# A second norm behind one block instead of two, three squares on another engine, and three pads that shift every working tile in SBUF

## The chip, the cores and the metric

The kernel runs on one core of a Trainium2 chip. The metric is device microseconds (us) of one execution. The engines are TensorE (PE, whose weight loads the profile lists apart as PEld), VectorE (DVE), ScalarE (ACT), GpSimd (POOL), and SyncE (SP), which here only issues DMAs. Each works off its own queue in order.

## The reference

One layer of a decoder trunk on x of 1024 positions and 1024 channels, all in float32:

```python
h = rms_norm(x, norm_mix_pre)
z = h @ w_in                                   # pool, query, RWKV and gate columns
merged = gates[0]*y_pool + gates[1]*y_rwkv + gates[2]*y_mem
x = x + rms_norm(merged @ w_o, norm_mix_post)  # the residual of the mixer
h = rms_norm(x, norm_ffn_pre)
u = causal_dwconv(h @ w_ffn_up, conv_w, conv_b)
u_gate, u_val = split(u)
f = (gelu(u_gate) * u_val) @ w_ffn_down
x = x + rms_norm(f, norm_ffn_post)
```

y_pool is causal pooling, y_rwkv a recurrence over 16 heads (run here in chunks of 64 positions), y_mem attention into 256 memory tokens.

## The kernel before

Everything is transposed: channels on the 128 partitions, positions along a row, in two halves of 512 positions. Each float32 operand is split into a high part, rounded to the format that TensorE takes at its fast rate (FR, float32r), and a low part, the remainder. A product is three matmuls (`mm3`, L167 to L169): high weights by high rows, high weights by low rows, low weights by high rows, each 128x128 by 128x512. A block is one 128-channel output over all 1024 input channels: 8 pieces of 128 channels, so 24 such matmuls into one bank of PSUM (`psg`).

Weights come in pieces of 128x256 (`load_w`, `load_more`): SP loads `wraw`, ACT casts it to `whi` (L128), POOL subtracts to get `wlo` (L131). There are two classes of buffers, used by turns, each with 3 `wraw`, 4 `whi` and 4 `wlo`; a block is four pieces.

The stages, by time in the trace: up to about 100 us the first norm of x; to about 1000 us the input projection (rows `hh`, `hl`) as filler between the small matmuls of the recurrence; then attention, and the projections of the branches (rows `oh`/`ol`, `ph_`/`pl_`, `yh`/`yl`), the merge (`mgh`/`mgl`) and the output projection `wo_gemm`; from about 1380 us the first FFN blocks one by one on rows `h2h`/`h2l`; from about 1510 to 1850 us the other FFN blocks in pairs (`up_pair`: seven products of 12 matmuls into banks `psf`, with weights `wt` and rows `h2h`/`h2l` or differences `t`); then the down projection (banks `psd`, weights `u`, rows `f`).

Around the change, for the second half of the positions: `wo_gemm(1, ...)` makes eight output blocks. Of each, VectorE copies the bank to the tile `o` (L1116), ScalarE squares the bank (L1090), and VectorE adds the square into `ss` (L1091). `wo_residual(1, ...)` has one matmul with `ones` sum `ss` over the channels (`norm`, L1096, into `psn`), ScalarE takes a logarithm and an exponential (L199, `rs`), and then for each of eight rows VectorE scales (L1134) and adds x (L1136), ScalarE squares, and VectorE adds into `s2` (L1091, `s` in the trace). It is a generator that stops after every second row. `wo_norm(1, ...)` sums `s2` by another L1096 matmul, scales again and splits into `h2h[1]`, `h2l[1]`. While this runs, TensorE makes the blocks of the FFN on the first half: `first(0)`, `first(NF)`, `first(1)`, `first(NF + 1)`, `first(2)`, `first(NF + 2)`, called f0, g0, f1, g1, f2, g2 below. Each is evacuated by `conv`: ACT (L961), then two DVE operations and a tiny copy (L962, L963, L965). The L1096 matmuls are pinned behind the matmul that was last when they were written.

SBUF is given out in pools. `const`, `wp` (weights, staging) and the pools of each stage (`rw`, `at`, `ow`, `fa` and others) are stacked from the low end; `hp`, `pmp`, `hf`, `yp` and others from the high end. What a matmul reads lies, in the program as built, at these places modulo 256 bytes (all offsets inside these tiles are multiples of 256):

| operands | before | after |
|---|---|---|
| `whi`, `wlo` (pool `wp`) | 192 | 224 |
| `hh`, `hl`, `yh`, `yl`, `mgl`, `h2h`, `h2l` (high end) | 224 | 224 |
| `mgh`, `oh`, `ol`, `ph_`, `pl_` | 64 | 224 |
| `wt` of `up_pair`: two of every six products in `ow`, the other four in `pmp` | 64, 224 | 224, 224 |
| `t` of `up_pair`: `T1`, `T2` in `at`, `T3` in `pmp` | 64, 64, 224 | 224 |
| `u`, `f` of the down projection (pool `at`) | 64 | 224 |
| `ones`, `ident`, `bonesr`, `cent` (`const`) | 192 | 192 |

Of the 512-wide three-matmul products, 3776 matmuls read weights at 192 and rows at 224 (2784 with `hh`/`hl`, 480 with `h2h`/`h2l`, 384 with `yh`/`yl`, 128 with `mgl`), 640 weights at 192 and rows at 64 (`mgh`, `oh`, `ol`, `ph_`, `pl_`), and of the 1428 into `psf` 648 read weights and rows at different places, 780 at the same. All 876 into `psd` read both at 64.

Of the kernel before, what the change touches and what calls it, by code (L numbers as in the profile page):

```python
# [9 lines left out]
F32 = mybir.dt.float32  # L10
FR = mybir.dt.float32r
AF = mybir.ActivationFunctionType
ALU = mybir.AluOpType
# [4 lines left out]
P = 128  # L18
# [10 lines left out]
NF = 22  # L29
# [15 lines left out]
def trunk_kernel(ctx: ExitStack, tc: tile.TileContext, xT, memT, pvec, w_in, w_kv, w_upd, w_upg,  # L45
                 w_pool, w_ppool, w_pmem, w_prwkv, w_o, w_fup, w_fdn, out):
    nc = tc.nc
    V, A, G, PE, SP = nc.vector, nc.scalar, nc.gpsimd, nc.tensor, nc.sync

    const = ctx.enter_context(tc.tile_pool(name="const", bufs=1))  # L50
# [54 lines left out]
                        base=-1, channel_multiplier=-1)  # L105
    G.memset(smask, 1.0)
    G.memset(smask.rearrange("p (c s) -> p c s", s=C)[:, :, 0:1], 0.0)
    eps = const.tile([P, 3], F32, name="eps")
    for j, e in enumerate((NORM_EPS, L2_EPS, LNX_EPS)):
        G.memset(eps[:, j:j + 1], e)  # L110
# [190 lines left out]

    def shifted(m, dst):

        zc = wp.tile([P, 1], F32, name="zc", tag="zc", bufs=4)

        def evac(t0, ps):
            d = dst[:, t0:t0 + 512]
            A.activation(d, ps, AF.Identity, scale=omu[:, m:m + 1])
            if t0 == 0:
                V.tensor_copy(zc, ps[:, 511:512])  # L310
            else:
                V.scalar_tensor_tensor(d[:, 0:1], zc, col("mu", m), d[:, 0:1], op0=ALU.mult,
                                       op1=ALU.add)
            V.scalar_tensor_tensor(d[:, 1:512], ps[:, 0:511], col("mu", m), d[:, 1:512],  # L314
                                   op0=ALU.mult, op1=ALU.add)
        return evac
# [532 lines left out]
    for hd in range(4):  # L849
        for t0, _ in HALVES:  # L850
            s = slice(t0, t0 + 512)
            q = as_.tile([P, 512], F32, name="q", tag="q", bufs=2)
            SP.dma_start(q, d_zq[hd][:, s])
            qh = as_.tile([P, 512], FR, name="qh", tag="qh")
            ql = as_.tile([P, 512], FR, name="ql", tag="ql")
            split(q, qh, ql, V)
            po = pss.tile([P, 512], F32, name="po", tag="s")
            for u in range(2):
                ps = psg.tile([P, 2, 256], F32, name="psco", tag="g0")
                for tt in range(2):  # L860
                    ts_ = slice((2 * u + tt) * P, (2 * u + tt + 1) * P)
                    mm3(ps[:, tt], (qh[:, ts_], ql[:, ts_]), (kh[:, hd], kl[:, hd]), True, True)
                mx = as_.tile([P, 8], F32, name="mxs", tag="mxs", bufs=2)
                V.reduce_max(mx[:, 0:2], ps, axis=AX.X)
                V.tensor_scalar(mx[:, 2:4], mx[:, 0:2], -SC, None, op0=ALU.mult)
                pr = as_.tile([P, 2, 256], F32, name="prb", tag="prb", bufs=2)
                for tt in range(2):
                    act(pr[:, tt], ps[:, tt], AF.Exp, bias=mx[:, 2 + tt:3 + tt], scale=SC,
                        accum_out=mx[:, 4 + tt:5 + tt])
                V.reciprocal(mx[:, 6:8], mx[:, 4:6])  # L870
                V.tensor_tensor(pr, pr, mx[:, 6:8].unsqueeze(2).broadcast_to([P, 2, 256]), op=ALU.mult)
                pt = (psc if u else psk).tile([P, 2, 2, P], F32, name="ptr", tag="c" if u else "k")
                for tt in range(2):
                    for m in range(2):
                        PE.transpose(pt[:, m, tt], pr[:, tt, m * P:(m + 1) * P], ident)
                pth = as_.tile([P, 2, 256], FR, name="pth", tag="pth", bufs=2)
                ptl = as_.tile([P, 2, 256], FR, name="ptl", tag="ptl")
                split(pt.rearrange("p m t s -> p m (t s)"), pth, ptl, V)
                for m in range(2):
                    mm3(po[:, u * 256:(u + 1) * 256], (vh[:, hd, m], vl[:, hd, m]), (pth[:, m], ptl[:, m]),  # L880
                        m == 0, m == 1)
            split(po, oh[hd][:, s], ol[hd][:, s], V)
        pool_products(hd)
        if hd < 2:
            pool_sums(hd + 2)
        for j, ev in fill[2 * hd:2 * hd + 2]:
            in_block(j, ev, 1)
# [197 lines left out]
    def sumsq(acc, src, first, eng):  # L1085
        if first:
            A.activation(acc, src, AF.Square)
        else:
            sq = wp.tile([P, 512], F32, name="sq", tag="st", bufs=3)[:, :src.shape[-1]]
            A.activation(sq, src, AF.Square)  # L1090
            eng.tensor_tensor(acc, acc, sq, op=ALU.add)  # L1091
# [13 lines left out]
    def wo_gemm(n, js):  # L1105
        s = slice(n * 512, n * 512 + 512)
        for j in js:
            if j == 0:
                o = [(ow if n == 0 else ow1).tile([P, 2, 512], F32, name="o", tag=f"q{4 * n + a}") for a in range(4)]
                os_.append([o[k // 2][:, k % 2] for k in range(KC)])  # L1110
                sss.append(ow.tile([P, 512], F32, name="ss", tag="ss", bufs=2))
            rhs = lambda k: (mgh[k][:, s], mgl[n][k])
            if n == 1 and j == 0:
                two.extend(two_gemms([load_w(w_o[e], KC) for e in range(2)], rhs, KC - 1))
            ps = two.pop(0) if two else gemm(load_w(w_o[j], KC), rhs)
            V.tensor_copy(os_[n][j], ps)  # L1116
            sumsq(sss[n], ps, j == 0, V)

    def wo_residual(n, after=None):

        s = slice(n * 512, n * 512 + 512)
        o = os_[n]
        rs = norm(ow, sss[n], after)
        s2 = ow.tile([P, 512], F32, name="s2", tag="ss", bufs=2)
        if n:
            xts = hf.tile([P, KC, 512], F32, name="xts", tag="h2h1")
            SP.dma_start(xts, xT[:, s].rearrange("(k p) t -> p k t", p=P))
        for k in range(KC):
            if n:
                xt = xts[:, k]  # L1130
            else:
                xt = ow.tile([P, 512], F32, name="xt", tag="xt", bufs=2)
                SP.dma_start(xt, xT[k * P:(k + 1) * P, s])
            V.scalar_tensor_tensor(o[k], o[k], col("g_mix_post", k), rs, op0=ALU.mult,  # L1134
                                   op1=ALU.mult)
            V.tensor_tensor(o[k], o[k], xt, op=ALU.add)  # L1136
            SP.dma_start(d_x1[k][:, s], o[k])
            sumsq(s2, o[k], k == 0, V)
            if k % 2:
                yield s2  # L1140
# [31 lines left out]
    s2 = next(res)  # L1172
# [12 lines left out]
    def first(j):  # L1185
        return up_block(j, 0, load_w(w_fup[j], KC))

    pairs = [[first(0), first(NF)]]
    res = wo_residual(1, last_mm[0])
    s2 = next(res)  # L1190
    for i in (1, 2):
        pairs.append([first(i)])
        s2 = next(res)
        pairs[i].append(first(NF + i))
        s2 = next(res, s2)

# [412 lines left out]
```

## Time and profile before

| | us |
|---|---|
| median of 3 runs (2083.38 to 2085.0) | 2084.89 |
| profiled execution, its own time | 2084.65 |
| span of its instructions | 2082.7 |
| PE busy (12246 matmul records) | 2026.5, 97% of the span |
| DVE, ACT, POOL busy | 1358.2, 1070.6, 810.8 |
| mean granted TensorE clock | 0.993 |

Of the time of an execution, 1.95 us lie outside the span. The profile says of busy PE that the ends of matmuls are modelled, since they are pipelined: how fast matmuls follow each other is read from the starts of rows in the timeline, not from the duration column.

### The profile page before, as it was taken

To read this page: it belongs to the slowest core of one execution; us is meant where nothing else is said; L and a number is where in the kernel's file an instruction comes from. 1 tells how busy PE (TensorE), PEld (TensorE's weight loads), DVE (VectorE), ACT (ScalarE), POOL (GpSimd) and SP (SyncE) were. 2 spreads that over 40 slices of the span, in tenths; PEclk is the share of its full clock that TensorE was granted. 3 is DMA by queue.
4 is the path that set the end of the run, shared out by engine and by line. 5 is a ranking of instruction groups with operands and counts; after the bars stand their busy time and mean duration, and the time that the engine had idled before them with its cause. 6 is when DMAs were issued, how large, how long until landed. Compare 5 with 4: busy or idle time off the path is not lost.

```text
span 2082.7 us, 34125 instructions
## 1 busy us (share of the span) xinstructions
PE 2026.5 (97%) x12246; PEld 1559.1 (75%) x12246; DVE 1358.2 (65%) x2167; ACT 1070.6 (51%) x2252; POOL 810.8 (39%) x917
## 2 busy tenths in 40 slices
PE   8999999999999999999999999998999999999997
PEld 5777767776778667876878878776778877777886
DVE  6567437664667357833795452769877777777798
ACT  7585348623772368434566243545443444444644
POOL 5521213121222121212122355565578888842341
PEclk9999999999999999999999999999999999999999
DMA  4312211120212021213526443634222222169766
GB/s 155 129 41 74 67 51 67 67 82 22 87 61 89 30 92 44 86 55 120 172 84 223 129 134 107 220 102 151 94 88 83 82 78 76 61 185 273 168 178 152
DMA packets 176713, 221.83 MB, mean 107 GB/s; under 512 B 16544, under 2 KB 128288, under 8 KB 176544
## 3 DMA queue, kind: packets, MB, share of 16 engines
q1 hardware_dynamic: 163616, 204.44, 30.2%
q0 software_dynamic: 11856, 14.16, 4.2%
q8 instruction: 97, 1.59, 0.3%
q10 hardware_dynamic: 1072, 1.05, 0.1%
q14 instruction: 72, 0.59, 0.1%
HBM read 170.30 MB, written 49.28 MB: 105 GB/s over the span
## 4 chain that ended last, share of the span: by engine, by line
PE 36%; DVE 5%; DMA 4%; POOL 3%; issue 2%; ACT 2%; SPq 1%; POOLq 0%; ACTq 0%; DVEq 0%
PE psg L167 6%; PE psg L169 6%; PE psg L168 6%; PE psf L169 3%; PE psf L167 3%; PE psf L168 3%; POOL wt L1027 2%; PE psd L168 2%; PE psd L169 2%; PE psd L167 2%; DMA R<-d_f 1%; POOL sm L1012 1%; DMA a<-in_w_fup 1%; ACT d L1043 1%; DMA fw<-in_w_fdn 1%
## 5 line engine op out<-in xcount | busy, mean ns | idle before, releaser
L131 POOL TENSOR_TENSOR wlo<-wraw,whi 128x256 fp32r<-128x256 f32 x472 | 410.4, 878 | 951.7 <-ACT whi L128 760.2
L167 PE MATMUL psg<-hh,whi 128*128 128x512 f32 x928 | 383.6, 413 | 2.5 <-DVE kv L314 2.5
L169 PE MATMUL psg<-hh,wlo 128*128 128x512 f32 x928 | 379.8, 409 | 0.1
L168 PE MATMUL psg<-hl,whi 128*128 128x512 f32 x928 | 378.8, 408 | 0.0
L128 ACT CAST whi<-wraw 128x256 fp32r<-128x256 f32 x472 | 182.7, 403 | 227.9 <-PE psg L168 122.1
L167 PEld LDWEIGHTS psg<-hh,whi 128*128 128x128 f32 x928 | 174.6, 188 | 46.5 <-DVE kv L314 3.8
L169 PEld LDWEIGHTS psg<-hh,wlo 128*128 128x128 f32 x928 | 174.3, 188 | 45.9 <-POOL wlo L131 5.1
L168 PEld LDWEIGHTS psg<-hl,whi 128*128 128x128 f32 x928 | 174.7, 188 | 42.9 <-issue 3.6
L1027 POOL TENSOR_TENSOR wt<-a,wt 128x256 fp32r<-128x256 f32 x136 | 133.8, 1012 | 30.8 <-ACT wt L1026 30.8
L167 PE MATMUL psd<-f,u 128*128 128x512 f32 x292 | 115.0, 394 | 5.7 <-ACT f L1347 3.4
L168 PE MATMUL psd<-f,u 128*128 128x512 f32 x292 | 115.0, 394 | 1.0 <-DVE f L1351 1.0
L169 PE MATMUL psd<-f,u 128*128 128x512 f32 x292 | 114.3, 393 | 0.4 <-DVE u L1351 0.4
L1027 POOL TENSOR_TENSOR wt<-sm,wt 128x256 fp32r<-128x256 f32 x102 | 106.8, 1067 | 14.6 <-ACT wt L1026 14.6
L169 PE MATMUL psf<-h2h,wt 128*128 128x512 f32 x272 | 108.0, 397 | 0.4 <-POOL wt L1027 0.3
L168 PE MATMUL psf<-h2l,wt 128*128 128x512 f32 x272 | 107.0, 393 | 0.0
L167 PE MATMUL psf<-h2h,wt 128*128 128x512 f32 x272 | 106.8, 393 | 0.0
L1026 ACT CAST wt<-sm 128x256 fp32r<-128x256 f32 x102 | 37.9, 404 | 128.2 <-POOL sm L1012 124.2
L1045 DVE SCALAR_TENSOR_TENSOR d<-z,pv,d 128x1023 f32<-128x1023 f32 x68 | 91.6, 1347 | 12.0 <-ACT d L1043 9.5
L169 PE MATMUL psf<-t,wt 128*128 128x512 f32 x204 | 81.3, 399 | 1.9 <-POOL wt L1027 1.9
L168 PE MATMUL psf<-t,wt 128*128 128x512 f32 x204 | 80.3, 394 | 0.0
L167 PE MATMUL psf<-t,wt 128*128 128x512 f32 x204 | 80.2, 393 | 0.0
L685 DVE TENSOR_TENSOR HV<-ph,Hd 64x128 f32<-64x128 f32 x112 | 32.3, 289 | 71.8 <-PE ph L639 47.7
(422 smaller groups left out, 4751.3 us busy)
## 6 DMA issues: line engine op xcount, KB each, us to landing
wraw<-in_w_in SPq DMA_DIRECT2D x240, 128.0 KB, 2.3
a<-in_w_fup SPq DMA_DIRECT2D x128, 128.0 KB, 2.4
d_zg<-st SPq DMA_DIRECT2D x48, 256.0 KB, 2.7
wraw<-in_w_fup SPq DMA_DIRECT2D x80, 128.0 KB, 2.4
fw<-in_w_fdn SPq DMA_DIRECT2D x33, 256.0 KB, 4.5
fraw<-d_f SPq DMA_DIRECT2D x33, 256.0 KB, 5.2
wraw<-in_w_prwkv SPq DMA_DIRECT2D x64, 128.0 KB, 2.4
wraw<-in_w_o SPq DMA_DIRECT2D x64, 128.0 KB, 2.5
```

The lines of the kernel that those rows point to most:

```text
L128: last_whi[0] = A.copy(hi, src).ins
L131: (V if lo_on_dve[0] else G).tensor_tensor(lo, src, hi.bitcast(F32), op=ALU.subtract)
L167: first = PE.matmul(ps, wh, xh, start=start, stop=False)
L168: PE.matmul(ps, wh, xl, start=False, stop=False)
L169: last_mm[0] = PE.matmul(ps, wl, xh, start=False, stop=stop).ins
L685: ready = V.tensor_tensor(HV[q, :, c + 1, e], ph[q], Hd[q], op=ALU.add).ins
L1012: eng.tensor_tensor(out_[u], a[u], b[u], op=op)
L1026: A.copy(w[0][:, us], src[u])
L1027: last_low[0] = G.tensor_tensor(w[1][:, us], src[u], w[0][:, us].bitcast(F32), op=ALU.subtract).ins
L1043: A.activation(d, z, AF.Identity, scale=col("cw2", j), bias=col("cb", j))
L1045: V.scalar_tensor_tensor(d[:, n:], z[:, :T - n], col(cw, j), d[:, n:], op0=ALU.mult, op1=ALU.add)
```

## The change

Three pads move places in SBUF: an unused tile `cpad` of 32 bytes a partition in `const` (all that follows in `const`, and `wp`, moves up 32 bytes), eight `zc` instead of four (32 bytes each as placed; what is stacked above moves another 128), and 128 bytes instead of 32 for `mxs` (two of them; the tiles of the attention above them move by 352 in all). The table above has the places that follow.

In `wo_gemm`, the squares of output blocks 5, 6 and 7 of the second half are taken by VectorE from the copy `o` in SBUF, not by ScalarE from the bank.

`wo_residual(1, ...)` is started behind f0 instead of behind g0, and its four parts follow f0, g0, f1, g1 instead of g0, f1, g1, f2.

```diff
+    const.tile([P, 8], F32, name="cpad")
...
-        zc = wp.tile([P, 1], F32, name="zc", tag="zc", bufs=4)
+        zc = wp.tile([P, 1], F32, name="zc", tag="zc", bufs=8)
...
-                mx = as_.tile([P, 8], F32, name="mxs", tag="mxs", bufs=2)
+                mx = as_.tile([P, 32], F32, name="mxs", tag="mxs", bufs=2)
...
             V.tensor_copy(os_[n][j], ps)
-            sumsq(sss[n], ps, j == 0, V)
+            if n == 1 and j > 4:
+                sq = wp.tile([P, 512], F32, name="sq", tag="st", bufs=3)
+                V.tensor_tensor(sq, os_[n][j], os_[n][j], op=ALU.mult)
+                V.tensor_tensor(sss[n], sss[n], sq, op=ALU.add)
+            else:
+                sumsq(sss[n], ps, j == 0, V)
...
-    pairs = [[first(0), first(NF)]]
+    pairs = [[first(0)]]
     res = wo_residual(1, last_mm[0])
+    s2 = next(res)
+    pairs[0].append(first(NF))
     s2 = next(res)
     for i in (1, 2):
         pairs.append([first(i)])
-        s2 = next(res)
+        s2 = next(res, s2)
         pairs[i].append(first(NF + i))
         s2 = next(res, s2)
```

TensorE at the norm of the second half, before (`psg_14031` is the bank of g0, `psg_14104` that of f1):

```order
L169 MATMUL psg_14031<-h2h0_13607,wlo_14026 128x512
L167 MATMUL psg_14031<-h2h0_13607,whi_14025 128x512
L168 MATMUL psg_14031<-h2l0_13608,whi_14025 128x512
L169 MATMUL psg_14031<-h2h0_13607,wlo_14026 128x512
L1096 MATMUL psn_14061<-ss_13496,ones_85 128x512
L167 MATMUL psg_14104<-h2h0_13607,whi_14080 128x512
L168 MATMUL psg_14104<-h2l0_13608,whi_14080 128x512
L169 MATMUL psg_14104<-h2h0_13607,wlo_14081 128x512
```

and after (`psg_13977` is the bank of f0, `psg_14050` that of g0; L1097 is the old L1096):

```order
L170 MATMUL psg_13977<-h2h0_13608,wlo_13972 128x512
L168 MATMUL psg_13977<-h2h0_13608,whi_13971 128x512
L169 MATMUL psg_13977<-h2l0_13609,whi_13971 128x512
L170 MATMUL psg_13977<-h2h0_13608,wlo_13972 128x512
L1097 MATMUL psn_14007<-ss_13497,ones_85 128x512
L168 MATMUL psg_14050<-h2h0_13608,whi_14026 128x512
L169 MATMUL psg_14050<-h2l0_13609,whi_14026 128x512
L170 MATMUL psg_14050<-h2h0_13608,wlo_14027 128x512
```

The norm's matmul moved ahead of the 24 matmuls of g0; nothing else on TensorE moved.

ScalarE from the square of output block 5 on, before (`sq` are the squares of blocks 5, 6, 7; `whi` the casts of weights; `ug` the evacuation of f0, `uv` that of g0; `rs` the logarithm and exponential of the norm):

```order
L1090 ACTIVATE sq<-psg 128x512
L128 CAST whi<-wraw 128x256 x4
L1090 ACTIVATE sq<-psg 128x512
L128 CAST whi<-wraw 128x256 x4
L1090 ACTIVATE sq<-psg 128x512
L128 CAST whi<-wraw 128x256 x4
L961 ACTIVATE ug<-psg,pv 128x512
L128 CAST whi<-wraw 128x256 x4
L961 ACTIVATE uv<-psg,pv 128x512
L199 ACTIVATE rs<-psn,eps 128x512
L199 ACTIVATE rs<-rs 128x512
```

and after, from the square of block 4 on:

```order
L1091 ACTIVATE sq<-psg 128x512
L129 CAST whi<-wraw 128x256 x16
L962 ACTIVATE ug<-psg,pv 128x512
L200 ACTIVATE rs<-psn,eps 128x512
L200 ACTIVATE rs<-rs 128x512
L129 CAST whi<-wraw 128x256 x2
```

Three squares are gone, and `rs` stands right behind `ug`: the four casts of g1 and the evacuation `uv` of g0 are now behind it.

VectorE from the copy of output block 7 to the first rows of the residual, before:

```order
L1116 COPY o<-psg 128x512
L1091 TENSOR_TENSOR ss<-ss,sq 128x512
L962 SCALAR_TENSOR_TENSOR ug<-psg,pv,ug 128x511
L963 SCALAR_TENSOR_TENSOR ug<-psg,pv,ug 128x510
L965 COPY zc_14001<-psg 128x2
L962 SCALAR_TENSOR_TENSOR uv<-psg,pv,uv 128x511
L963 SCALAR_TENSOR_TENSOR uv<-psg,pv,uv 128x510
L965 COPY zc_14056<-psg 128x2
L1134 SCALAR_TENSOR_TENSOR o<-o,pv,rs 128x512 x2
L1136 TENSOR_TENSOR o<-o,xts 128x512 x2
```

and after:

```order
L1117 COPY o<-psg 128x512
L1120 TENSOR_TENSOR sq<-o 128x512
L1121 TENSOR_TENSOR ss<-ss,sq 128x512
L963 SCALAR_TENSOR_TENSOR ug<-psg,pv,ug 128x511
L964 SCALAR_TENSOR_TENSOR ug<-psg,pv,ug 128x510
L966 COPY zc_14002<-psg 128x2
L1140 SCALAR_TENSOR_TENSOR o<-o,pv,rs 128x512 x2
L1142 TENSOR_TENSOR o<-o,xts 128x512 x2
```

A multiplication came in, and the rows of the residual start one evacuation earlier; between its rows there are still three evacuations, now those of g0, f1, g1, before those of f1, g1, f2. SP issues the same DMAs; the eight writes of the residual to `d_x1` stand four weight pieces further up, 20 instead of 24 FFN pieces ahead of the first. POOL's order is the same.

## The prediction

> **What bounds the kernel.** I read the page first, then the waits of TensorE over the whole span, then busy times by stage.
>
> ```profile
> PE 2026.5 (97%) x12246; PEld 1559.1 (75%) x12246; DVE 1358.2 (65%) x2167; ACT 1070.6 (51%) x2252; POOL 810.8 (39%) x917
> ```
>
> ```profile
> PE psn L1096 <- DVE s L1091: 8.3, 1, 8.3
> ```
>
> ```profile
> 0.00:100.00 100.00, 89.81 (x338) 64.96 (x339) 62.06 (x89) 67.81 (x112) 52.51 (x97) 0.98 0.44 147
> 100.00:300.00 200.00, 198.66 (x1644) 146.98 (x1642) 118.04 (x232) 101.46 (x221) 37.73 (x46) 1.00 0.16 52
> 1260.00:1380.00 120.00, 120.00 (x515) 96.06 (x514) 68.28 (x87) 57.09 (x128) 69.88 (x82) 1.00 0.48 150
> 1520.00:1700.00 180.00, 179.14 (x772) 144.08 (x771) 131.69 (x142) 80.02 (x169) 155.90 (x164) 1.00 0.23 77
> ```
>
> (stretch, its length, then busy us of PE, PEld, DVE, ACT, POOL, clock, DMA share, GB/s.) TensorE is the bound from 100 us on: 199 of 200, 120 of 120, 179 of 180 us. The one long wait is 8.3 us at the second-half norm, which the moved code touches. So two things count: how fast matmuls follow each other, and that one wait.
>
> **The places.** The duration column hides the first; the starts in TensorE's timeline show it. A `psg` stretch on `hh`, one on `mgh`, four product starts of the first `up_pair`, and a stretch of the down projection:
>
> ```profile
> 316.68 0.40 PE L167 MATMUL psg<-hh,whi 128*128 128x512 f32 x1
> ...
> 320.18 0.39 PE L167 MATMUL psg<-hh,whi 128*128 128x512 f32 x1
> ...
> 1340.05 0.39 PE L167 MATMUL psg<-mgh,whi 128*128 128x512 f32 x1
> ...
> 1344.91 0.39 PE L167 MATMUL psg<-mgh,whi 128*128 128x512 f32 x1
> ...
> 1514.06 0.39 PE L167 MATMUL psf<-t,wt 128*128 128x512 f32 x1
> ...
> 1516.86 0.39 PE L167 MATMUL psf<-h2h,wt 128*128 128x512 f32 x1
> ...
> 1519.62 0.39 PE L167 MATMUL psf<-t,wt 128*128 128x512 f32 x1
> ...
> 1522.34 0.40 PE L167 MATMUL psf<-h2h,wt 128*128 128x512 f32 x1
> ...
> 1930.27 0.39 PE L167 MATMUL psd<-f,u 128*128 128x512 f32 x1
> ...
> 1935.71 0.39 PE L167 MATMUL psd<-f,u 128*128 128x512 f32 x1
> ```
>
> The first two rows lie 15 matmuls apart: 3.50/15 = 233.3 ns each, weights at 192 and rows at 224. The `mgh` rows lie 21 apart: 231.4 ns (192 with 64, every third row 224). Then three `up_pair` products of 12 matmuls, same lines, same engine load: product 3 (T2 at 64, weights at 224) 2.80/12 = 233.3; product 4 (B21 and weights at 224) 230.0; product 5 (T3 and weights at 224) 226.7. The down projection, both at 64, 24 apart: 226.7. All at full clock and width. Operands at one place modulo 256 run at 226.7, or 230.0 just behind an unequal product; at two places, at 231 to 233. After the change all these operands lie at 224, so I take 226.7 for all; the other end is 230.0, as if the neighbouring product were not the reason for it.
>
> Where the matmuls are (first figure with x, records into `psg`, then `psf`):
>
> ```profile
> 0.00:100.00 100.00, 79.28 (x306) 59.03 (x307) 13.01 (x23) 15.90 (x26) 0.98 0.44 147
> 100.00:1000.00 900.00, 643.76 (x2372) 426.15 (x2371) 32.83 (x63) 65.52 (x98) 1.00 0.21 69
> 1346.00:1415.00 69.00, 68.41 (x290) 53.95 (x289) 11.00 (x19) 7.85 (x12) 1.00 0.44 141
> 1415.00:1510.00 95.00, 82.49 (x337) 63.87 (x336) 22.52 (x38) 11.51 (x15) 0.95 0.37 117
> 1510.00:1850.00 340.00, 333.08 (x1423) 265.04 (x1421) 67.05 (x101) 19.58 (x34) 1.00 0.24 80
> ```
>
> Weights at 192 with rows at 224: 3776 x 6.6 ns = 24.9 us. Weights at 192 with rows at 64: 640 x 4.7 = 3.0. In `psf`, 648 unequal x 6.6 = 4.3, and 780 equal ones rid of slow neighbours, mean 228 to 226.7, 1.0. Together 33.2 us of TensorE time. What of it reaches the end:
> - 1346 to 1415 us, 290 x about 6.2 ns = 1.8 us: nothing. It lies ahead of the long wait, which another chain ends.
> - Up to 100 us, about 1.7: half, since TensorE stands still for 10 of these 100 us. Minus 0.8.
> - 100 to 1000 us, 2372 x 6.6 = 15.7: filler between the small matmuls of the recurrence. One step:
>
> ```profile
> 300.44 0.26 ACT L668 COPY HV<-pu 64x128 f32<-64x128 f32 x1 [1.00 <-DVE HV L667]
> 300.80 0.39 PE L167 MATMUL psg<-hh,whi 128*128 128x512 f32 x1
> 301.12 0.45 PE L639 MATMUL ph<-HV,BKN 128*64 128x64 f32 x8
> ```
>
>  HV is ready at 300.70, its reader starts at 301.12 because the filler ahead of it started at 300.80: 0.4 us of slack against 4 fillers x 6.6 = 0.03 us. Some steps are tighter; I take off 15%, 2.4 us.
> - The rest of `psg` (27.9 - 1.7 - 15.7 - 1.8 = 8.7 us): weights come by rings through DMA, ACT and POOL with room (POOL 70 of 120 us). Minus 10%, 0.9.
> - `psf`, 5.3: POOL is at 156 of 180 us there. Minus 15%, 0.8.
>
> Sum: 33.2 - 1.8 - 0.8 - 2.4 - 0.9 - 0.8 = **26.5 us** gained. The lower end is 230.0 for all: 3776 x 3.3 + 640 x 1.4 + 648 x 3.3 = 15.5, less the same fifth, 12. The upper end takes off only what lies ahead of the wait: 31.4. The matmuls with `ones`, `ident`, `cent`, `bonesr` (192) read unequal places before and after, apart from the first norm's 32 records. Nothing else of a pad costs time: `cpad` is never written, and `zc` and `mxs` are written as before.
>
> **The norm and the squares.** ACT, DVE and TensorE at the long wait:
>
> ```profile
> 1392.16 0.77 ACT L961 ACTIVATE ug<-psg,pv 128x512 f32<-128x512 f32 x1
> 1396.49 0.41 ACT L128 CAST whi<-wraw 128x256 fp32r<-128x256 f32 x1 [2.65 <-DMA wraw<-in_w_fup]
> 1396.81 0.78 ACT L961 ACTIVATE uv<-psg,pv 128x512 f32<-128x512 f32 x1
> 1397.48 0.68 ACT L199 ACTIVATE rs<-psn,eps 128x512 f32<-128x512 f32 x1
> 1398.19 0.63 ACT L199 ACTIVATE rs<-rs 128x512 f32<-128x512 f32 x1
> ```
>
> ```profile
> 1387.98 0.84 DVE L1091 TENSOR_TENSOR ss<-ss,sq 128x512 f32<-128x512 f32 x1 [3.34 <-ACT sq L1090]
> 1394.42 0.15 DVE L965 COPY zc<-psg 128x2 f32<-128x2 f32 x1
> 1399.13 1.89 DVE L1134 SCALAR_TENSOR_TENSOR o<-o,pv,rs 128x512 f32<-128x512 f32 x2
> ...
> 1421.54 1.80 DVE L1091 TENSOR_TENSOR s<-s,sq 128x512 f32<-128x512 f32 x2
> ```
>
> ```profile
> 1391.68 1.02 PE L1096 MATMUL psn<-ss,ones 128*128 128x512 f32 x2
> 1414.69 0.39 PE L169 MATMUL psg<-h2h,wlo 128*128 128x512 f32 x1
> 1423.40 2.08 PE L1096 MATMUL psn<-s,ones 128*128 128x512 f32 x2 [8.32 <-DVE s L1091]
> 1428.68 0.50 PE L169 MATMUL psg<-h2h,wlo 128*128 128x512 f32 x1
> ```
>
> The norm's matmul is done at 1392.7, but its logarithm runs at 1397.48: in ACT's queue it stands behind casts that wait for weights (until 1396.49) and behind `uv`. Then VectorE works from 1399.13 to 1423.34 without a gap, and TensorE, out of blocks since 1415.08, waits for it.
>
> The three multiplications on VectorE (about 0.9 us each: 0.84 for an addition, 1.89 for two scalings) replace waits of 3.3 us for ScalarE's squares, the row at 1387.98: cost nothing. Without them the move would fail: f0 ends 24 matmuls ahead of 1391.68, at 1386.1, while `ss` is complete at 1388.82. Now it follows the copy of block 7, whose bank is done when f0 starts (1380.5): copy, product and sum, 0.8 to 1.3 us each, end from 1383.0 to 1384.3, 2 us early. If DVE's wait for the square of block 4 ate these, TensorE would lose some of 2 us that the later wait gives back.
>
> `rs` now runs behind `ug`: 1392.83 to 1394.1, and VectorE is free at 1394.57. So the chain of 24.2 us, with the same 23 operations and three evacuations, starts at 1394.6 in place of 1399.13 and ends 4.5 us earlier, near 1418.8. The ring of weights ahead of `ug` stays. Behind `rs` are now the casts of g1 and `uv`, and the casts from then on wait for VectorE's rows one block earlier in TensorE's terms. g1's third piece, behind a square, comes near 1398.1, and TensorE wants it at 1400.5: 2 us of cover. If it goes, TensorE waits ahead of the long wait, at no cost.
>
> The wait also costs clock:
>
> ```profile
> 1245.00:1250.00 5.00, 2.42 (x7) 1.36 (x6) 0.69 (x1) 3.45 (x6) 2.10 (x3) 0.80 0.21 67
> 1410.00:1420.00 10.00, 5.08 (x22) 3.75 (x20) 10.00 (x14) 4.51 (x10) 4.49 (x6) 0.93 0.43 139
> 1420.00:1430.00 10.00, 6.60 (x16) 4.58 (x17) 7.77 (x14) 7.28 (x14) 4.25 (x5) 0.55 0.69 215
> ```
>
> From 1423.4 to about 1429 matmuls ran at half rate: 2.7 us lost. A wait of 2.6 us at 1245 also cost some clock (0.80 over 5 us). With the chain ending at 1418.8 and TensorE out of work at 1413.3 (1.8 us of place gain), a wait of 5.5 us is left: it still costs clock, and I count 0.5 us gained, between 0 and 1.5. This term: **5.0 us**, between 2.5 (the chain stretched 2 us by POOL's use of the same moments) and 6.
>
> **Sum.** 26.5 + 5.0 = 31.5; 2084.65 - 31.5 = 2053.2, against the profiled execution, 0.24 us below the median. I forecast **2053 us**.
>
> **Rivals.**
> - *The recurrence binds.* If the steps from 100 to 1000 us wait for ACT and DVE and not for filler, three quarters of that gain turn into waits: 13.3 falls to 4, the time is 2062. Against it: the slack above; for it: DVE and ACT work between every two small matmuls.
> - *The long wait only changes its cause.* If weights for g1 or f2 come late by the whole gain, 2084.65 - 26.5 = 2058. Against it: the 2 us of cover.
> - *Place means nothing in `psg`.* The 233 ns would belong to that stage (weights of 256 columns, two classes), and only 5.0 remain: 2079.6. The three `up_pair` products on the same lines speak against it. The Trainium skill (TensorE: Matmul & The Clock Gate, "Wait — 56ns, not 53.3ns?") speaks for it: start to start is the column count over the clock plus about 2.5 ns, 215.7 ns at 512, with no word of places. By that rule the pads do nothing and this rival's time holds. The trace disagrees: two rates at one width and full clock.
> - *Slower: all at 224.* Now ACT, POOL, DVE and DMAs also write at the place that TensorE reads. If that delays matmuls beyond 233.3 ns, the pads cost: from 5.0 us / 5064 matmuls = 1.0 ns above it the kernel is slower, and at 6.6 ns above, 2113. Against it: the down projection reads at 64 what ACT and DVE write at 64, at 226.7.
>
> **Chances.** Forecast 0.68, recurrence 0.16, changed cause 0.06, no place effect 0.06, slower 0.04. The range runs from 2046 (31.4 + 5.5 gained, and some more from 256-wide products) to 2068 (12 + 4.5 gained); it holds the recurrence and the changed cause, and leaves out the last two. A change of 0.2%, 4.2 us, is about what a measurement of this kernel can tell from none. Faster by more 0.93, within 0.03, slower 0.04.
>
> **What would show it.** In the profile after: starts of `psg` rows 226 to 228 ns apart in long stretches, and all `up_pair` products alike; the down projection's unchanged. The first residual row near 1394.6 less what was gained by then, and the wait at the second `psn` 4 to 6 us instead of 8.3. Wrong would be: `psg` starts still 233 apart (no place effect), or small matmuls of the recurrence with waits on ACT HV and DVE that add up to 10 us (recurrence).

## The result, and the profile after

| | before | after |
|---|---|---|
| median of 19 executions, us | 2084.43 | 2079.82 (2074.02 to 2083.55) |
| ratio to before, 95% interval | | 0.9981 (0.9974 to 0.9988) |
| span of the profiled execution | 2082.7 | 2080.0 |

The forecast was 2053, the range 2046 to 2068. The kernel is 0.19% faster, about what can be told from no change. On a second chip the same change gave 0.9972 (0.9961 to 0.9983). The profiled execution after is 2 us above the median. One execution of the kernel before (3222.78 us) and one of `pads_alone` below (4909.27 us) lie far outside all others and are left out of the times here.

The matmuls did get faster. The page after, first part, and then starts in TensorE's timeline (a `psg` run on `hh`, one on `mgh`, and products of the first `up_pair`):

```profile
PE 2014.5 (97%) x12246; PEld 1558.7 (75%) x12246; DVE 1361.4 (65%) x2170; ACT 1069.4 (51%) x2249; POOL 812.5 (39%) x917
```

```profile
315.31 0.39 PE L168 MATMUL psg<-hh,whi 128*128 128x512 f32 x1
...
316.70 0.39 PE L168 MATMUL psg<-hh,whi 128*128 128x512 f32 x1
...
318.74 0.39 PE L168 MATMUL psg<-hh,whi 128*128 128x512 f32 x1
...
1333.53 0.39 PE L168 MATMUL psg<-mgh,whi 128*128 128x512 f32 x1
...
1336.25 0.39 PE L168 MATMUL psg<-mgh,whi 128*128 128x512 f32 x1
...
1502.59 0.39 PE L168 MATMUL psf<-t,wt 128*128 128x512 f32 x1
...
1510.75 0.39 PE L168 MATMUL psf<-t,wt 128*128 128x512 f32 x1
...
1515.26 0.50 PE L168 MATMUL psf<-h2h,wt 128*128 128x512 f32 x1 [1.60 <-ACT wt L1027]
```

`mgh`: 12 apart, 2.72/12 = 226.7 ns; it was 231.4. The products: 36 apart, 8.16/36 = 226.7; before, they went at 226.7 to 233.3. But in the product behind them TensorE stands still for 1.60 us, waiting for weights. The first pair of rows (6 apart, 1.39/6 = 231.7) lies just behind small matmuls, the second (9 apart, 2.04/9 = 226.7) further on in the same run; more on that under the recurrence.

TensorE's waits after, over the span (the longest, for `px` near the start, left out), and the stretch around the second psn:

```profile
PE psd L168 <- ACT f L1355: 4.8, 2, 4.1
PE psf L170 <- POOL wt L1028: 4.0, 11, 0.6
PE psn L1097 <- DVE s L1092: 3.7, 1, 3.7
```

```profile
1405.00:1415.00 10.00, 6.32 (x21) 4.13 (x20) 5.85 (x11) 4.15 (x10) 5.55 (x7) 0.83 0.65 204
```

The long norm wait fell from 8.3 to 3.7 us, and with it the clock loss (0.83 over 10 us, where before 0.55 stood). In its place the start of the down projection waits longer, and weights for the products come late; before, these two rows were:

```profile
PE psd L167 <- ACT f L1347: 3.4, 2, 2.7
PE psf L169 <- POOL wt L1027: 2.3, 9, 0.4
```

(The longer wait at the down projection belongs to this execution: in the second one of the table below that stretch is as long as before.)

So TensorE needs less and the end hardly moves. To see where it went, I took the starts of the same matmuls in both traces and cut the execution at six of them. The table has the length of each stretch, in us; places in the span of before (the expectations below count from TensorE's first matmul, 5.2 us into the span). Line numbers after are 1 to 8 higher than before. "After, 2nd" is another profiled execution of the same change, from the second chip.

| stretch | before | after | after, 2nd | gain forecast | gain measured |
|---|---|---|---|---|---|
| 5 to 105, first norm | 100.2 | 100.4 | 100.0 | 0.8 | -0.2, 0.2 |
| 105 to 1005, recurrence with filler | 899.8 | 894.3 | 895.3 | 13.3 | 5.5, 4.5 |
| 1005 to 1350, attention, projections | 345.2 | 341.4 | 341.1 | 5.7 | 3.8, 4.1 |
| 1350 to 1517, norm, single FFN blocks | 166.9 | 167.5 | 167.9 | 7.2 | -0.6, -1.0 |
| 1517 to 1848, products in pairs | 331.5 | 335.8 | 330.8 | 4.5 | -4.3, 0.7 |
| 1848 on, down projection | 222.7 | 224.5 | 222.7 | 0 | -1.8, 0.0 |

(The forecast's 31.5 us split by stretch; the `psg` remainder by its share of matmuls. In the third stretch most of the measured gain is not the places': three kernels of the next section, whose matmuls there ran at the old pace or nearly so, had 340.2 to 342.3 us. In the fifth, the same kernel after took 335.8 and 330.8 us in two executions, so a difference of up to 5 us there need not come from the kernel.)

### The profile page after: what moved, and what is told of

Same layout as the page of the kernel before. It is cut to its first block, busy times and chain, and to the rows that moved or that the text cites. A ratio compares the mean times of both kernels' runs of the same rounds, so it can differ in the third digit from the quotient of the medians.

```text
span 2080.0 us, 34125 instructions
## 1 busy us (share of the span) xinstructions
PE 2014.5 (97%) x12246; PEld 1558.7 (75%) x12246; DVE 1361.4 (65%) x2170; ACT 1069.4 (51%) x2249; POOL 812.5 (39%) x917
## 4 chain that ended last, share of the span: by engine, by line
PE 30%; DVE 7%; DMA 5%; POOL 4%; issue 4%; ACT 3%; SPq 0%; POOLq 0%; ACTq 0%; DVEq 0%
PE psg L170 5%; PE psg L169 5%; PE psg L168 5%; POOL wt L1028 2%; PE psd L169 2%; PE psd L170 2%; PE psf L170 2%; PE psd L168 2%; PE psf L169 2%; PE psf L168 2%; POOL sm L1013 1%; DMA a<-in_w_fup 1%; DMA g<-d_zg 1%; DMA R<-d_f 1%; POOL wlo L132 1%
```

## The experiments

Each ratio stands against the kernel before on the same chip; since the rows come from three chips, compare kernels by their ratios. The stretches are those of the table, in one profiled execution of each kernel: A 5 to 105, B 105 to 1005, C 1005 to 1350, D 1350 to 1517, E 1517 to 1848, F from there to the start of TensorE's last matmul. `whole_change` is the kernel after once more; the other labels are explained one by one.

| kernel | median us | ratio, interval | A | B | C | D | E | F |
|---|---|---|---|---|---|---|---|---|
| pads_alone | 2075.21 | 0.9963 (0.9950 to 0.9976) | 100.9 | 895.2 | 341.0 | 167.1 | 331.9 | 222.7 |
| move_alone | 2082.66 | 1.0000 (0.9992 to 1.0009) | 101.0 | 899.7 | 342.3 | 167.9 | 331.1 | 224.0 |
| whole_change | 2076.48 | 0.9972 (0.9961 to 0.9983) | 100.0 | 895.3 | 341.1 | 167.9 | 330.8 | 222.7 |
| norm_first | 2074.48 | 0.9961 (0.9949 to 0.9973) | 97.8 | 894.6 | 340.9 | 165.2 | 333.4 | 224.1 |
| sum_before | 2068.24 | 0.9932 (0.9920 to 0.9945) | 100.4 | 900.4 | 341.2 | 164.8 | 321.6 | 221.8 |
| sum_on_dve | 2057.61 | 0.9878 (0.9865 to 0.9891) | 99.6 | 896.3 | 339.2 | 167.2 | 316.2 | 221.5 |
| pads_and_sum | 2056.90 | 0.9879 (0.9866 to 0.9893) | 99.5 | 895.1 | 339.0 | 165.2 | 316.4 | 222.7 |
| both_fixes | 2053.06 | 0.9861 (0.9846 to 0.9877) | 99.3 | 895.2 | 339.3 | 164.6 | 315.7 | 221.0 |
| norm_clear | 2052.42 | 0.9859 (0.9844 to 0.9874) | 99.5 | 894.4 | 342.2 | 160.8 | 316.2 | 221.6 |
| scalar_squares | 2058.94 | 0.9885 (0.9871 to 0.9900) | 100.0 | 895.8 | 339.3 | 168.0 | 316.2 | 221.1 |
| less_filler | 2057.06 | 0.9881 (0.9864 to 0.9897) | 101.4 | 872.5 | 338.0 | 166.0 | 336.5 | 223.0 |
| far_places | 2082.23 | 1.0000 (0.9991 to 1.0009) | 99.8 | 899.4 | 340.2 | 167.0 | 331.8 | 224.5 |

**Which part of the change did it.** First the pads alone, then the move with the squares alone:

```diff
# pads_alone: before.py with cpad, zc bufs=8, mxs [P, 32]
# move_alone: after.py without these three
```

> Only the three pads; order and squares as before. Theory A (places shorten long runs of matmuls, other chains eat part of it): the start-to-start of long psg runs goes from 233 to 227 ns, the long norm wait stays at about 8.3 us, and the time equals that of the whole change, 2080 us (2077 to 2082). Theory B (the pads give nothing at the end, the moved norm gives the 4.6 us): 2084.4. Theory C (each gives about half): 2082.

> The moved norm and the three squares on VectorE, without the pads. Theory A: the first matmul of the second norm waits 4 to 5 us less, but its logarithm stands in ScalarE's queue behind a cast that waits for its weights, so that VectorE starts the normalised rows as late as before: 2084.4 us (2082.5 to 2086). Theory B: 2080. Theory C: 2082.

> The whole change once more, beside the others on one chip. Theory A: 0.998 of before, 2079 us on a chip where before takes 2083. If the loss of 4 us against the pads alone is real, it stays above the pads alone's 0.996.

The pads give 0.37% (7.6 us, somewhat more than theory A's), the move nothing, the whole 0.19 and 0.28%: theories B and C fall. That the whole is worse than the pads alone isn't shown, since the intervals overlap. TensorE's waits with the pads alone, and with the move alone:

```profile
PE psn L1097 <- DVE s L1092: 9.9, 1, 9.9
```

```profile
PE psn L1096 <- DVE s L1091: 3.3, 1, 3.3
...
PE psg L169 <- POOL wlo L131: 2.4, 3, 1.6
PE psg L167 <- ACT whi L128: 1.6, 2, 1.2
```

The pads make the norm wait longer (9.9), the move makes it shorter (3.3) and brings waits for weights in its place. Stretch D lasts 167 to 168 us in all of them and in before. Its matmuls in runs fell from 151.2 to 148.0 us: the 3 us became waiting.

**The norm's stretch.** The move did start the residual early: its first row on VectorE, at 1399.13 before, stands at 1385.67, of which 8.9 us had been gained by then. What follows is ScalarE's timeline after, then VectorE's first rows of the second norm and its last subtraction ahead of the products, after and before:

```profile
1410.34 0.77 ACT L962 ACTIVATE ug<-psg,pv 128x512 f32<-128x512 f32 x1
1411.01 1.01 ACT L129 CAST whi<-wraw 128x256 fp32r<-128x256 f32 x3
1416.13 0.41 ACT L129 CAST whi<-wraw 128x256 fp32r<-128x256 f32 x1 [4.11 <-PE psg L170]
1416.44 0.78 ACT L962 ACTIVATE uv<-psg,pv 128x512 f32<-128x512 f32 x1
1417.12 0.68 ACT L200 ACTIVATE rs<-psn,eps 128x512 f32<-128x512 f32 x1
...
1385.67 1.89 DVE L1140 SCALAR_TENSOR_TENSOR o<-o,pv,rs 128x512 f32<-128x512 f32 x2
...
1418.77 2.07 DVE L1159 SCALAR_TENSOR_TENSOR o<-o,pv,rs 128x512 f32<-128x512 f32 x3
...
1471.44 1.86 DVE L1255 TENSOR_TENSOR o<-o 128x512 f32<-128x512 f32 x2
```

```profile
1426.89 2.08 DVE L1153 SCALAR_TENSOR_TENSOR o<-o,pv,rs 128x512 f32<-128x512 f32 x3
...
1480.01 1.86 DVE L1247 TENSOR_TENSOR o<-o 128x512 f32<-128x512 f32 x2
```

13.5 us early at 1385, the chain is 8.1 us early at the second norm's rows and 8.6 at its last subtraction. The 5 us went in ScalarE's queue: the second `rs` stands behind the last cast of the block NF+3, which comes 4.1 us after its neighbours. The profile puts that wait down to TensorE, but the matmuls that had read the cast's buffer before, those of g2, were over by 1406. More likely it is the load: `wraw` has three buffers, so the fourth piece is loaded only when GpSimd is done with the first, and in norm_first, below, the same cast waits for the DMA of `wraw`. From there VectorE works without a gap, and the casts of later blocks stand behind splits that wait for it. So I put `rs` ahead of that cast:

```diff
-    ahead = [load_w(w_fup[3], KC), load_w(w_fup[NF + 3], KC)]
+    ahead = [load_w(w_fup[3], KC)]
     steps = wo_norm(1, s2, last_mm[0])
     next(steps)
+    exp = phase[1][-1]
+    ahead.append(load_w(w_fup[NF + 3], KC))
+    later(last_whi[0], exp, True)     # order only
```

> The whole change, and the logarithm of the second norm ahead of the one weight cast of the block NF+3 that waited for its ring (1412.0 to 1416.1 in the trace after). Theory A: rs starts near 1412.5 instead of 1417.1, VectorE's chain from there to about 1475 comes 4 to 4.5 us earlier, and the time falls by 3 to 4.5 us against the whole change, to 2075.5 to 2077. Rival D (the product stage's weight loop or the transfers at the start of the down projection set the end): the 4.5 us show at 1475 but not at the end, 2080.

```profile
1409.81 0.68 ACT L200 ACTIVATE rs<-psn,eps 128x512 f32<-128x512 f32 x1
1410.52 0.63 ACT L200 ACTIVATE rs<-rs 128x512 f32<-128x512 f32 x1
1413.86 0.41 ACT L129 CAST whi<-wraw 128x256 fp32r<-128x256 f32 x1 [2.71 <-DMA wraw<-in_w_fup]
1414.29 1.28 ACT L194 ACT_TABLE_LOAD   x1
1415.58 1.14 ACT L122 CAST h2h<-o 128x512 fp32r<-128x512 f32 x2
```

ScalarE's timeline of norm_first: `rs` came 4.5 us earlier against what precedes it, as expected, but the late cast now stands between `rs` and the first splits `h2h`, and some 3 of the 4.5 us are lost there: from the end of `rs` to the first split it is 4.4 us, where after had 1.3. D fell by 2.3 and 2.7 us against the two profiles of the whole change, not by 4.5. The time, 0.9961, lies below the whole change's 0.9972 and 0.9981, but its interval overlaps with both, and part of its profile's gain is in stretch A, which the edit doesn't touch. So the next kernel puts the first two splits ahead of the late cast as well (together with the sum below, as both_fixes has the sum):

```diff
-    later(last_whi[0], exp, True)
+    later(last_whi[0], hi, True)      # hi: cast of the second split of wo_norm
...
+            if n == 0:                # first cast of block 4, too
+                later(whis[-4], hi, True)
```

> The whole change with the sum on VectorE, and behind the logarithm of the second norm directly the first two splits of the normalised rows: the late cast of the block NF+3 and the casts of the next block come after them in ScalarE's queue. Theory A (the stretch from 1345 to 1512 us of the kernel before lasts 164.6 to 167.9 us in every kernel so far, because ScalarE's queue lets VectorE's chain start late; the earlier edit only put the late cast ahead of the splits): the chain comes 4 to 5 us earlier, the stretch falls to 161 to 162.5 us, 2050 to 2052 us against 2053 with the earlier edit. Rival G (VectorE's chain and the weight ring behind it bind in any case): 164.6 as before, 2053.

```profile
1412.47 0.68 ACT L202 ACTIVATE rs<-psn,eps 128x512 f32<-128x512 f32 x1
1413.18 0.63 ACT L202 ACTIVATE rs<-rs 128x512 f32<-128x512 f32 x1
1414.90 1.28 ACT L122 CAST h2h<-o 128x512 fp32r<-128x512 f32 x2 [1.09 <-DVE o L1161]
1416.09 0.40 ACT L130 CAST whi<-wraw 128x256 fp32r<-128x256 f32 x1
```

Now the splits follow `rs` with 1.1 us between, and D is 160.8 us, where it was 164.6 with the half edit: the queue on ScalarE was what held this stretch, and rival G falls. TensorE's waits between the two matmuls that start at 1430 and 1485 before, 8.7 us in the kernel after, are down to 1.9. In whole times the two can't be told apart (0.9859 and 0.9861): in the profile 3 of the 3.8 us went in C, which lasted 342.2 in place of 339.3, and that the edit can't reach. The same order without the moved norm was not run, so what the move itself is worth stays open: with the sum of the next section, D is 165.2 without the move and 167.2 with it.

**The products in pairs.** GpSimd makes the low parts of the weights there, and two sums of weights (the second is a difference). One edit moves the first sum to VectorE, on both kernels:

```diff
-        both(G, sm, a21, a22, ALU.add)
+        both(V, sm, a21, a22, ALU.add)
```

> The whole change, and the first sum of weights of each pair of FFN blocks (two of 0.74 us) taken by VectorE instead of GpSimd. Theory A (the pairs run at GpSimd's rate, 17.9 us of work and 2.3 us of waits per pair, not at TensorE's 84 x 0.2267 = 19.0): a pair goes from 20.2 to 19.1 to 19.4 us, some ten pairs gain 0.8 to 1 us each, 2070 to 2073 us if the down projection lets it through. Rival E (the loop runs through ScalarE's casts behind activations that wait for VectorE): the same pair time or a longer one, 2080 to 2084.

> The kernel before, with the first sum of weights of each pair on VectorE, without pads and move. Theory A (with GpSimd relieved the pairs run at TensorE's pace, and that hangs on the places): 84 x 0.2307 = 19.4 us a pair in place of 19.8, the 10.6 us of waits in the product stage fall to about 1, 2073 to 2075 us. Theory F (the places mean nothing in that stage): all of what the same edit gave on the whole change, 20 us and more, 2061 to 2064.

> The pads and the sum on VectorE, without the move and the squares. Theory A: the pads alone took 2075.9; of the 15.3 us of waits in their product stage about 14.4 go: 2060 to 2062 us. If instead the moved norm helps once GpSimd is relieved, the version with the move (2057.6) is faster by 3 to 4 us.

> The whole change with both edits: the logarithm of the second norm ahead of the late cast, and the sum on VectorE. Theory A (the two waits lie in different stages and add): 2053 to 2054.5 us. Rival D (what comes earlier at 1475 is lost at the start of the down projection): 2057.5.

The same 300 us of busy times, of before, after, sum_before and sum_on_dve:

```profile
1520.00:1820.00 300.00, 297.70 (x1271) 236.69 (x1270) 220.07 (x238) 132.90 (x282) 260.04 (x272) 1.00 0.23 75
```

```profile
1520.00:1820.00 300.00, 296.39 (x1271) 235.47 (x1271) 223.11 (x240) 134.87 (x285) 258.50 (x267) 1.00 0.23 76
```

```profile
1520.00:1820.00 300.00, 300.00 (x1302) 244.46 (x1301) 254.14 (x280) 147.18 (x302) 255.31 (x253) 1.00 0.23 76
```

```profile
1520.00:1820.00 300.00, 300.00 (x1325) 248.43 (x1324) 255.35 (x282) 142.89 (x300) 259.32 (x250) 1.00 0.24 79
```

Before and after TensorE starts 1271 matmuls in 300 us, whatever the places, while a pair of 84 matmuls at 226.7 ns would take 19.04. With one sum moved off GpSimd it starts 1302 with the old places, 1325 with the new. The mean hides two phases. The table has the time from one pair's start to the next, and GpSimd's lead: by how much the last low part of a pair's fourth product was finished ahead of that product's start, both in us:

| pair | 2 | 3 | 4 | 5 | 6 | 7 | 8 | 9 to 16 |
|---|---|---|---|---|---|---|---|---|
| before, time | 19.51 | 19.48 | 19.40 | 19.25 | 19.14 | 19.35 | 19.88 | 20.13 to 20.29 |
| before, lead | 5.0 | 4.3 | 3.4 | 2.6 | 1.6 | 0.6 | 0.0 | 0.0 to 0.1 |
| after, time | 19.04 | 19.04 | 19.04 | 19.04 | 19.57 | 20.17 | 20.15 | 20.12 to 20.36 |
| after, lead | 4.7 | 3.5 | 2.2 | 1.1 | 0.0 | 0.0 | 0.0 | 0.0 |
| sum_on_dve, time | 19.04 | 19.04 | 19.04 | 19.04 | 19.04 | 19.04 | 19.04 | 19.04 |
| sum_on_dve, lead | 5.2 | 5.4 | 5.8 | 5.1 | 5.3 | 5.6 | 5.7 | 4.9 to 6.5 |

The first pairs go at TensorE's pace, which the places set; each eats a part of GpSimd's lead. When it is gone, GpSimd's loop sets the pace, about 20.2 us a pair with either kernel, and faster first pairs only bring that moment forward, from pair 8 to pair 6. In the kernel after, the moved sum and the low parts stood so on GpSimd, the last row with the sum on VectorE:

```profile
L1013 POOL TENSOR_TENSOR sm<-a,a 128x256 f32<-128x256 f32 x28 | 20.6, 737 | 7.6 <-DMA a<-in_w_fup 5.9 <-POOL sm L1013 1.7
L1028 POOL TENSOR_TENSOR wt<-sm,wt 128x256 fp32r<-128x256 f32 x89 | 94.9, 1086 | 12.7 <-ACT wt L1027 12.7
...
L1028 POOL TENSOR_TENSOR wt<-sm,wt 128x256 fp32r<-128x256 f32 x93 | 107.5, 1175 | 16.4 <-ACT wt L1027 16.4
```

(count, then busy us, mean ns, and the idle time before them.) The edit took 20.6 us of work off GpSimd in 300 and the 7.6 us of waits ahead of it; which of the two counted isn't separated. Stretch E tells it in time: 331.5 to 321.6 without the pads, 335.8 and 330.8 to 316.2 with them. Starts that follow within 260 ns, the others taken as 227, add up to 320.9, 316.8, 320.7 and 315.3 us, and the rest of each stretch, the waits, to 10.6, 19.0, 0.9 and 0.9. So the pads gave TensorE 4 to 5 us here, and the waits took it; where GpSimd leaves the way free, the places are worth 321.6 - 316.2 = 5.4 us in E, for which the prediction counted 5.3 ahead of its deduction.

On the whole change the sum brought 20 us, twice what was expected: E alone fell by 15 to 20, to 19.04 us a pair. On the kernel before it gave 14.2 us, more than the 10 of E: in the profiles D is 2.1 us shorter, F 0.9, and C, which the edit doesn't touch, 4.0. Why D and F are shorter stays open. The sum brought more than expected with the pads alone, too: 2056.90, where 2060 to 2062 stood. Theory F (21 us without the pads) falls, and so does rival E, though VectorE went from 220 to 254 us busy in 300. Moved norm or not made no difference with the sum either (0.9878 and 0.9879). The norm's edit beside the sum gained 2.6 us in D, and both_fixes took 2053.06 us, nearer to Theory A than to rival D's 2057.5; but the intervals of 0.9861 and 0.9878 overlap, so that it comes through to the end isn't shown.

**The squares.** All squares by ScalarE again, with the move, the pads and the sum:

```diff
-            if n == 1 and j > 4:
+            if False:
```

> The whole change with the sum on VectorE, but all squares of the output blocks by ScalarE again. As the prediction has it, the sum of squares would then be complete some 2 to 3 us after the first block f0 is done, and TensorE waits at the moved norm; but as the stretch around it is bound by VectorE's chain, Theory A gives the same time within 2 us, 2056 to 2060. If the squares are what makes the move possible, 2 to 5 us slower, 2060 to 2063.

0.9885 (0.9871 to 0.9900) against 0.9878 (0.9865 to 0.9891): no difference shown; D is 168.0 against 167.2. The move works without them as well as with them.

**The recurrence.** Of the 24 matmuls of a filler block, two low-row products are left out (k = 3 and 5); the output of these blocks lacks them:

```diff
+            if log is not None and k in (3, 5):
+                m = PE.matmul(ps, ws[k][0], rhs(k)[0], start=False, stop=False)
+                last_mm[0] = PE.matmul(ps, ws[k][1], rhs(k)[0], start=False, stop=False).ins
```

> The whole change, with two low-row matmuls of every 24 left out in the 32 blocks of the input projection that fill the recurrence: 128 matmuls fewer. Theory A (TensorE sets the end of that stage, and the pads brought little there because half of the fillers stand near small matmuls, where the start-to-start is 230 to 340 ns whatever the places): 128 x 0.227 = 29 us go, 23 to 29 of them at the end. Rival H (the recurrence's chain over ScalarE and VectorE sets the end, and the fillers' shorter time turned into waits): 12 us or less.

The trace has 96 matmuls fewer, not 128: 24 of the 32 blocks pass through these lines. 96 x 0.227 = 21.8 us. Stretch B fell from 895.3 to 872.5, by 22.8: all of it. So TensorE sets the end of B and rival H falls, as does the prediction's rival that the recurrence binds. At the end 19 to 21 us arrive (0.9881 against 0.9972 and 0.9981). E lasted 336.5 us here, but 330.8 and 335.8 in the two profiles of the whole change, so a loss there isn't shown.

Why then did 2372 faster fillers bring B only 5 us? Because the places hardly show in the first fillers behind a small matmul. Six rows after, from a step of the recurrence:

```profile
301.08 0.45 PE L640 MATMUL pr<-HV,AR 128*64 128x64 f32 x8
301.46 0.50 PE L168 MATMUL psg<-hh,whi 128*128 128x512 f32 x1
301.80 0.40 PE L169 MATMUL psg<-hl,whi 128*128 128x512 f32 x1
302.03 0.40 PE L170 MATMUL psg<-hh,wlo 128*128 128x512 f32 x1
302.36 0.45 PE L640 MATMUL py<-AR,HV 64*64 64x64 f32 x8
302.74 0.50 PE L168 MATMUL psg<-hh,whi 128*128 128x512 f32 x1
```

The first filler behind a small matmul takes 340 ns to the next, the second 230. Over all of B, by a filler's place in its run of fillers (mean ns to the next filler, waits included; places 4, 5 and 8 to 11 left out):

| place in the run | count | before | after |
|---|---|---|---|
| 1st | 245 | 336.6 | 336.4 |
| 2nd | 161 | 230.2 | 233.0 |
| 3rd | 129 | 235.6 | 235.8 |
| 6th, 7th | 65 | 233.2 | 229.3 |
| 12th and later | 1220 | 234.4 | 228.1 |

The gain is in the 1220 that stand twelfth or later, about half of all fillers: 6.3 ns each, 7.7 us. Against it stand about 2 us of new waiting behind fillers ahead of small matmuls.

**Do distances matter, or only equality?** The pad in `const` made 160 bytes: weights, `mgh`, `oh`, `ph_`, `u`, `f` at 96, the high end still at 224.

```diff
-    const.tile([P, 8], F32, name="cpad")
+    const.tile([P, 40], F32, name="cpad")
```

> The whole change with a pad of 160 bytes instead of 32 in const: the weights and all pools stacked from the low end at 96 modulo 256, those from the high end at 224 as before. Theory A (only equality counts, at whatever place): hh, hl, yh, yl, h2h products (96 with 224) start 231 to 234 ns apart in long runs, those on mgh, oh, ph_ (96 with 96) and the down projection (96 with 96) 226.7; the time is that of the kernel before, 2080 to 2084 us. If the distance counts (128 apart instead of 32), the start-to-start differs from 233.

```profile
315.28 0.40 PE L168 MATMUL psg<-hh,whi 128*128 128x512 f32 x1
...
318.79 0.39 PE L168 MATMUL psg<-hh,whi 128*128 128x512 f32 x1
...
1140.13 0.39 PE L168 MATMUL psg<-oh,whi 128*128 128x512 f32 x1
...
1148.29 0.39 PE L168 MATMUL psg<-oh,whi 128*128 128x512 f32 x1
```

TensorE's starts of that kernel: `hh` at 224 with weights at 96, 3.51/15 = 234 ns; `oh` with weights at 96 both, 8.16/36 = 226.7, where before it was 231 to 233. Equality counts, at 96 as at 64 and 224. The time is that of before (1.0000), so it wasn't the pads as such that gave the 0.37%. One expectation failed: the merge's matmuls took 232.4 ns on the mean and not 226.7. Of each three, only the one on `mgl`, which stayed at 224, reads unequal places, but the starts behind all three lie 231 to 234 ns apart: one unequal matmul in three is enough to slow its neighbours.

## Why the prediction was wrong, point by point

Forecast were 31.5 us, measured 4.6 (on a second chip 6.0). The rate of the matmuls came out as predicted, and so did the earlier start of the norm's chain. What failed is the step from there to the end of the kernel: it took off between nothing and 15% for the other engines where they took back all of the gain (products, norm), and it gave one rate to matmuls of which nearly half don't have it (recurrence).

- **Places: right in the rate.** Equal places modulo 256 gave 226.7 ns in `psg` and in every product. The rival that places mean nothing falls. The pitch that the Trainium skill gives for this width (TensorE: Matmul & The Clock Gate, "Wait — 56ns, not 53.3ns?"), 215.7 ns, isn't what this trace shows: it has two rates, 226.7 and 231 to 234 ns, at one width and full clock, told apart by places. The slower rival falls, too: no long run was slower with all tiles at 224.
- **The recurrence, 13.3 us: mis-sized, 4.5 to 5.5 measured.** The step "2372 x 6.6 = 15.7" took a rate from a long run and gave it to every filler. Nearly half of them stand among the first eleven of their run, where the places matter little or not at all. The rival had the size (4) by luck, with another cause, and less_filler shows that cause wrong: TensorE does bind there.
- **The products, 4.5 us: 0.7 and -4.3 measured.** The step that failed is "minus 15%" for POOL at 156 of 180 us. I had read TensorE as the bound from "179 of 180 us busy" beside it. The busy column can't tell: it was 297.70 of 300 while GpSimd set the pace in most of them, and 300.00 when TensorE did. The window was badly chosen, too: 1520 to 1700 is mostly the pairs that GpSimd's lead carries, and the pairs from 1645 on are the slow ones. The Trainium skill (Perfetto Trace Analysis, "Identifying the Most-Contended Engine") says that matmul occupancy is no good measure of how near TensorE is to its limit, since matmuls are pipelined, and names the busy share of weight loads as one. Over 1520 to 1820 the trace agrees: 78.9% before, 78.5% after, 81.5% and 82.8% with the sum moved. In the prediction's own windows it would not have helped: 144.08 of 180 and 96.06 of 120 are 80.0% both. The same page of the Trainium skill, in "Optimizing Scalar/DVE Operations", warns that work passed between GpSimd and VectorE might not help, since they share a read port; here it brought 14 to 20 us, though GpSimd's low parts from `sm` went from 1086 to 1175 ns on the mean.
- **The norm, 5.0 us, and the `psg` around it: nothing measured.** Right were the earlier `rs`, the chain's earlier start (4.6 us beyond the places' gain; forecast 4.5), the shorter wait and less half-rate clock. The failed step is "If it goes, TensorE waits ahead of the long wait, at no cost": I followed the queue behind the first `rs` and not behind the second. The late cast there holds `rs` (4.1 us), and TensorE's waits came behind the norm, 7.8 us more of them between the matmuls of 1430 and 1485, where norm_clear has 1.0 more. The rival "the long wait only changes its cause" described this, but kept the whole place gain beside it.
- **The squares "without which the move would fail": wrong**, by scalar_squares.
- **The 1005 to 1350 stretch, 5.7 us: 0 to 3 arrive.** The failed step is "minus 10%" for the rings of weights. TensorE's matmuls got faster as counted: the starts behind 512-wide matmuls, taken as for E above, add up to 282.3 us before and 276.6 after. But move_alone and sum_before, with the old places, last 342.3 and 341.2 us there with 8.3 and 8.4 us of waits, and the kernels with the 32-byte pad 338.0 to 342.2 with 10.8 to 13.7. Part of that is one wait, at 1245 in the trace before, and it isn't for weights but for the rows of the merge:

```profile
PE psg L167 <- ACT mgh L121: 2.6, 1, 2.6
...
PE psg L167 <- ACT mgh L121: 0.6, 1, 0.6
```

  The first row is of the profile before, the second of move_alone. In the ten profiles with the 32-byte pad it took 2.0 to 3.1 us. Since the profile before has it, too, at the old places, it isn't shown that the faster matmuls bring it.

## What to carry to other kernels

A gain on the busiest engine is worth, stage by stage, only the distance to the next chain; measure that distance before summing, by starts per time and not by a matmul's busy share, and over the end of the stage: its beginning can live on what another engine made ahead. A rate from a long run holds for long runs: look at the start-to-start where the counted instructions stand. And when a chain is started earlier, follow it to its second and third visit to each in-order queue: the cast that waited for a ring behind `rs` took back what the first visit had won.

The fastest version here, the whole change with the first sum on VectorE and the splits ahead of the late cast, takes 2052.42 us, 0.9859 of before (0.9844 to 0.9874); 14 of these 30 us the sum gives without the rest.

## What the hardware showed that I had not expected

- 512-wide matmuls directly behind a small one take 336 ns to the next whatever the places; in the 2nd and 3rd position it is 230 to 236; the place shows from about the sixth on.
- Places 128 apart cost on the mean as much as 32 apart (234.8 against 234.4 ns from the 12th filler on), but eight in ten of them spread from 229 to 241, where those 32 apart stay within 231 to 235.
- The half-rate windows of the clock in the two traces, but for the last at the program's end, take 3.41, 6.83 or 10.24 us, multiples of one length: 3.41 behind a wait of 2.7 us, 10.24 around the norm's of 8.3. Not every such wait is followed by one: the second profile of the change has a wait of 2.7 us for `mgh` and no half-rate window there.
